# Grouping the matmuls of a half weight chunk by width in a one-layer hybrid encoder trunk

## Chip, cores and metric

The kernel runs on one core of a Trainium2 chip, as one program that is launched once. The metric is the device time of one execution in microseconds (us). The engines are named as in the profile: PE is TensorE (the matmuls), PEld its weight loads, DVE is VectorE, ACT is ScalarE, POOL is GpSimd and SP issues the DMAs.

## What is computed

One layer of an encoder trunk on 256 tokens of width 2048, all in float32:

```
h    = rmsnorm(x, norm_mix);  proj = h @ w_in            # 2048 -> 6176 columns, the mixers' inputs
y    = concat(ssd_mixer(proj), gla_mixer(proj))          # 256 x 2048
x    = x + y @ w_out                                     # output projection, 2048 -> 2048
h    = rmsnorm(x, norm_ffn)
u    = causal_dwconv3(h @ ffn_w_up)                      # 2048 -> 2 x 5632
gate, val = split(u)
x    = x + (silu(gate) * val) @ ffn_w_down               # 5632 -> 2048
pg   = sigmoid(rmsnorm(x, norm_ple) @ ple_w_gate)        # 2048 -> 2048
x    = x + pg * (p @ ple_w_proj)
out  = rmsnorm(x, norm_final)
```

The change touches the four large products with `w_out`, `ffn_w_up`, `ffn_w_down` and `ple_w_gate`, that is, everything from the output projection on.

## The kernel before

**Tiling.** Activations lie transposed in the on-chip memory: 128 channels on the partitions, the 256 tokens along the free axis. Each weight matrix is cut into blocks of 128 x 128. One product (m, k) multiplies block (m, k) by the 128 input channels k and adds into output tile m, an accumulator `pm_t` of 128 x 512 in PSUM. There are four such accumulators.

**Two parts for each number.** Weights and activations are each split into a high part and a low part (the tiles `whi` and `wlo`; an activation tile is 128 x 2 x 256, high part first, low part second), and the matmuls take these split tiles. A product is then two matmuls in `mm2`: `whi` against both activation parts side by side, 512 columns wide (line 219, or line 222 for the last k of an output tile), and `wlo` against the high part alone, 256 columns wide, added into the first half of the accumulator (line 220). For the last k the narrow one comes first and the wide one last. Each matmul loads its own weights. The input projection and one output tile of the last stage (`single`) use `mm3` instead: three matmuls of 256 columns (lines 226 to 228).

**Weight stream.** A chunk is 16 blocks, 128 x 2048, fetched by one DMA into a `raw` tile (four of them). A half chunk is 8 blocks. For each half, ACT casts `raw` into `whi` (line 185, in `prepare`) and DVE subtracts to give `wlo` (line 186). There are five `whi` and five `wlo` buffers, so a cast has to wait until PE is done with the half chunk that stood in the buffer.

**Stages.** `project` walks a list of products made by `steps`, 16 per chunk. The last four k (five in the down projection) of the first two output tiles come after both tiles' other products, so that the activations which are finished last are needed late. The stages are: the output projection (256 products), then twice the up projection (704) and down projection (352) of one half of the hidden channels, then the gate projection (256, of which the last tile's 16 use `mm3`). That makes 2624 products, 2608 of them in `mm2`.

**Order around them.** The order of PE's instructions is the order of the program text; a scheduler at build time orders the other engines. When an output tile is whole, `evac` is called: it adds to the residual (line 917) and splits the sum for the next stage (lines 260 and 261), or, in the up projection, combines the two halves of the accumulator (lines 232 and 233), does the convolution and gating (lines 957 to 969) and splits the result (lines 267 and 268). Every four products `tick()` lets one waiting task put in its next piece. Here these are a norm's small matmuls (line 288, then line 321 six ticks later, and the copy of its result, line 331) and the loads of `p @ ple_w_proj` for the gate stage.

Of the kernel before, what the change touches and what calls it, by code (L numbers as in the profile page):

```python
# [15 lines left out]
T = 256  # L16
# [28 lines left out]
TICK = 4  # L45
# [36 lines left out]


def steps(n_m, n_k, tail):
    """(m, k) in the order of the products: the last k of the first two m come after both."""
    cut = n_k - tail
    s = [(m, k) for m in (0, 1) for k in range(cut)]
    s += [(m, k) for m in (0, 1) for k in range(cut, n_k)]
    return s + [(m, k) for m in range(2, n_m) for k in range(n_k)]


SEQ16 = steps(16, KT, 4)
SEQ_UP = steps(2 * UPH, KT, 4)
SEQ_DN = steps(16, UPH, 5)


@with_exitstack
def trunk(ctx, tc, wst, wv, xin, pin, prm_d, cst_d, gku_d, out):
    nc = tc.nc
    V, S, G, PE = nc.vector, nc.scalar, nc.gpsimd, nc.tensor  # L100
# [12 lines left out]
    def slot(dtype=F32, shape=(128, 512)):  # L113
        return gpool.tile(list(shape), dtype, name="slot")
# [4 lines left out]
    def pmt():  # L119
        return pm.tile([128, 512], F32, name="pm_t")  # L120

    def pxt():
        return px.tile([128, 512], F32, name="px_t")
# [1 line left out]
    def v3(ap, n):  # L125
        return ap.rearrange("p (a b) -> p a b", a=n)

# [1 line left out]
    now = [0]  # L129
    tasks = []  # L130
    done = {}
# [1 line left out]
    def tick():  # L133
        now[0] += 1
        for t in list(tasks):
            if t[0] <= now[0]:
                d = next(t[1], None)
                if d == 0:
                    continue
                if d is None:  # L140
                    tasks.remove(t)
                else:
                    t[0] = now[0] + d
                break
# [8 lines left out]
        while any(done.get(k, 1 << 30) > now[0] for k in keys):  # L153
            yield 0

# [1 line left out]
    ready = {}  # L157

    def raw_tile():
# [37 lines left out]
    def load(c):  # L197
        if c not in ready and c < N_CHUNK:
            ci = ORDER[c]
            with tc.high_priority(offset=PRIO):  # L200
                if c not in loaded:
                    fetch_ahead(c)
                ready[c] = prepare(loaded.pop(c), ci, 1)

    def chunk(c):
        load(c)
        load(c + 1)
        return ready.pop(c)

    def lhs(wt, j):  # L210
        hi, lo = wt[j // 8]
        w = slice((j % 8) * 128, (j % 8 + 1) * 128)
        return hi[:, w], lo[:, w]

    def mm2(ps, wt, j, act, first, last):
        hi, lo = lhs(wt, j)
        both = act.rearrange("p a t -> p (a t)")
        if not last:
            PE.matmul(ps, lhsT=hi, rhs=both, start=first, stop=False)  # L219
        PE.matmul(ps[:, 0:T], lhsT=lo, rhs=act[:, 0, :], start=False, stop=False)  # L220
        if last:
            PE.matmul(ps, lhsT=hi, rhs=both, start=False, stop=True)  # L222

    def mm3(ps, wt, j, act, first, last):
        hi, lo = lhs(wt, j)
        PE.matmul(ps, lhsT=hi, rhs=act[:, 0, :], start=first, stop=False)  # L226
        PE.matmul(ps, lhsT=hi, rhs=act[:, 1, :], start=False, stop=False)  # L227
        PE.matmul(ps, lhsT=lo, rhs=act[:, 0, :], start=False, stop=last)  # L228
# [5 lines left out]
        return t  # L234

    def project(base, seq, acts, n_k, evac, single=None):
        """Products of a weight stream in the order seq; evac(m, ps) when an output tile is whole."""
        ps = {}
        wt = None
        for n, (m, k) in enumerate(seq):  # L240
            if n % 16 == 0:
                wt = chunk(base + n // 16)
            if k == 0:
                ps[m] = pmt()
            if m == single:
                mm3(ps[m][:, 0:T], wt, n % 16, acts[k], k == 0, k == n_k - 1)
            else:
                mm2(ps[m], wt, n % 16, acts[k], k == 0, k == n_k - 1)
            if k == n_k - 1:
                evac(m, ps.pop(m))  # L250
            if n % TICK == TICK - 1:
                tick()

# [1 line left out]
    def pcol(i):  # L255
        return prm[:, i:i + 1]

# [73 lines left out]
        S.copy(out=keep, in_=ps)  # L331
        then(r, keep)

# [1 line left out]
    prm = const.tile([128, NPRM], F32, name="prm")  # L335
    x = const.tile([128, KT, T], F32, name="x")
    cst = const.tile([128, NCST], F32, name="cst")
# [33 lines left out]
    for m in range(KT):  # L371
        wt = ready[m // 8]
        if m % 2 == 0:
            ps = pmt() if m % 4 == 0 else pxt()
# [19 lines left out]
    for a in proj:  # L394
        store_proj(*a)

# [1 line left out]
    usuf_r = const.tile([128, 128], F32R, name="usuf_r")  # L398
    ones_r = const.tile([128, 128], F32R, name="ones_r")
    cbh = const.tile([128, 12], F32, name="cbh")  # L400
# [38 lines left out]
        S.activation(out=t, in_=c, func=AF.Tanh)  # L439
        V.scalar_tensor_tensor(out=out, in0=t, scalar=1.0, in1=c, op0=ALU.add, op1=ALU.mult)  # L440

# [1 line left out]
    gkl = const.tile([32, T], F32, name="gkl")  # L443
    G.memset(gkl, 1.0)
    dta = const.tile([128, 32], F32, name="dta")
# [73 lines left out]
        PE.matmul(ps[:, 16:32], lhsT=tri, rhs=a_tm[:, 16:32], start=True, stop=True)  # L519
        S.activation(out=esuf, in_=ps[:, 0:32], func=AF.Exp)  # L520

# [1 line left out]
    ssd_x = [None] * 8  # L523
    bT = slot()
    cT = slot()
# [194 lines left out]
                    mix[i] = split(y)  # L720
            yield from norm_task(ssd_sq[g], 512, then, 9)

# [1 line left out]
    gq = [slot(), slot()]  # L724
    gk = [slot(), slot()]
    gla = {}
# [119 lines left out]
        V.tensor_tensor(out=o, in0=o, in1=sg, op=ALU.mult)  # L846
        mix[8 + i] = split(o)

# [1 line left out]
    def ev_in(kind, i, ps):  # L850
        if kind == "conv":
            ev_conv(i, ps)
        elif kind == "q":
            ev_qk(gq, i, ps, 128.0 ** -0.5)
        elif kind == "k":
            ev_qk(gk, i, ps, 1.0)
            mark(("k", i))
        elif kind == "z":
            ev_z(i, ps)
        else:  # L860
            ev_g(i, ps)

    vps = None
    for ci, (kind, i) in enumerate(PLAN):
        if ci == 0:
            late_loads()
        if ci > 2:
            wt = chunk(N_PROJ + ci)
        else:
            wt = ready.pop(N_PROJ + ci)  # L870
# [14 lines left out]
        if kind == "v":  # L885
# [3 lines left out]
            for kk in range(4):  # L889
                k = kc * 4 + kk  # L890
                hi, lo = wt[kk // 2]
# [11 lines left out]
        else:  # L903
            ps = pmt()
# [6 lines left out]
    while tasks:  # L911
        tick()

# [1 line left out]
    def add_res(i, ps):  # L915
        for h in range(2):
            V.tensor_tensor(out=x[:, i, :], in0=x[:, i, :], in1=ps[:, h * T:(h + 1) * T], op=ALU.add)  # L917
# [8 lines left out]
    sq_ffn = SumSq()  # L926
    xf = [None] * KT
    project(OFF_OUT, SEQ16, mix, KT, residual(sq_ffn, P_GFFN, xf))

# [1 line left out]
    state.clear()  # L931

    def delayed(f):
# [42 lines left out]
    for half in range(2):  # L976
        base = OFF_F0 if half == 0 else OFF_F1
        project(base, SEQ_UP, xf, KT, ev_up(half))
        if half == 0:
            project(base + N_UP, SEQ_DN, hid, UPH, add_res)  # L980
        else:
            sq_ple = SumSq()
            project(base + N_UP, SEQ_DN, hid, UPH, residual(sq_ple, P_GPLE, xg))

# [1 line left out]
    state.clear()  # L986
    sq_fin = SumSq()
    emb = {}
# [52 lines left out]
    start(first_emb())  # L1041
    project(OFF_GATE, SEQ16, xg, KT, delayed(ev_gate), single=KT - 1)

# [1 line left out]
    banks = {}  # L1045

    def turn(q, c):
# [19 lines left out]
    with tc.high_priority(offset=PRIO):  # L1067
        v, t = [small.tile([128, 2], F32, name=n, bufs=2) for n in ("rv", "rt")]
# [105 lines left out]
```

## Time and profile before

| | us |
|---|---|
| device time, median of 3 runs (lowest to highest) | 1256.36 (1256.25 to 1256.43) |
| span of the profiled execution | 1254.4 |
| PE busy in it | 1243.2 (99%) |
| DVE busy | 896.0 (71%) |
| ACT busy | 691.2 (55%) |
| the four large projections, from the first wide matmul to the last | 313.25 to 1235.57 |

The profiled span leaves out about 1.9 us that the device time holds around it. Matmuls are pipelined: one that is listed with 0.40 us starts 0.23 us before the next. What a matmul costs is therefore read from the distance between two starts in the timeline, not from its listed duration.

### The profile page before, as it was taken

What the parts mean: (1) busy time and instruction counts of PE and PEld (TensorE: products, weight loads), DVE (VectorE), ACT (ScalarE), POOL (GpSimd) and SP (SyncE); (2) the same over time, 40 slices, a digit from 0 to 9 for tenths busy, and PEclk for the clock granted to TensorE, in tenths of its full rate; (3) what the DMA queues carried; (4) which work ended last, traced back from release to release, by engine and by line L of the source; (5) the groups of instructions that cost most, each with busy time, mean ns of one, the idle gap of its engine ahead of it and who ended that gap; (6) DMA issues with size and microseconds to landing.
All of it is one profiled execution on the core that took longest, in us unless ns stands there. A gap on an engine that the chain in (4) does not pass through costs nothing.

```text
span 1254.4 us, 19554 instructions
## 1 busy us (share of the span) xinstructions
PE 1243.2 (99%) x7707; PEld 1110.7 (89%) x7707; DVE 896.0 (71%) x1531; ACT 691.2 (55%) x1144; POOL 2.9 (0%) x10
## 2 busy tenths in 40 slices
PE   9999999999999999999999999999999999999997
PEld 7999999999888888888888888888888888888886
DVE  7877665788777787777775555777777776666775
ACT  8685564565545565555553333555555554444664
POOL 0000000000000000000000000000000000000000
PEclk9999999999999999999999999999999999999999
DMA  9745353344555455555555555555555555556531
GB/s 332 295 156 172 124 202 135 137 167 168 198 174 199 168 202 173 196 179 191 187 183 193 178 197 174 198 173 197 183 186 191 179 196 193 199 172 223 197 131 67
DMA packets 36830, 231.01 MB, mean 184 GB/s; under 512 B 4209, under 2 KB 4593, under 8 KB 11138
## 3 DMA queue, kind: packets, MB, share of 16 engines
q1 hardware_dynamic: 36738, 229.76, 52.4%
q8 instruction: 60, 0.98, 0.3%
q14 instruction: 32, 0.26, 0.1%
HBM read 225.55 MB, written 4.19 MB: 183 GB/s over the span
## 4 chain that ended last, share of the span: by engine, by line
PE 97%; DVE 1%; ACT 1%; DMA 1%; SPq 0%; issue 0%; DVEq 0%
PE pm_t L219 46%; PE pm_t L220 25%; PE pm_t L226 6%; PE pm_t L228 6%; PE pm_t L227 6%; PE pm_t L222 3%; PE pm_t L897 1%; PE pm_t L898 1%; PE pm_t L896 1%; DMA raw<-in_wst_dram 1%; PE px_t L629 1%; DVE wlo L186 0%; PE px_t L792 0%; ACT xg L260 0%; PE px_t L288 0%; ACT whi L185 0%
## 5 line engine op out<-in xcount | busy, mean ns | idle before, releaser
L185 ACT CAST whi<-raw 128x1024 fp32r<-128x1024 f32 (+3 forms) x444 | 444.2, 1005 | 513.8 <-PE pm_t L219 244.1
L186 DVE TENSOR_TENSOR wlo<-raw,whi 128x1024 fp32r<-128x1024 f32 (+3 forms) x444 | 517.1, 1168 | 273.3 <-ACT whi L185 270.5
L219 PE MATMUL pm_t<-xg,whi 128*128 128x512 f32 x1545 | 549.8, 398 | 0.0
L220 PE MATMUL pm_t<-xg,wlo 128*128 128x256 f32 x1648 | 446.0, 281 | 0.0
L219 PEld LDWEIGHTS pm_t<-xg,whi 128*128 128x128 f32 x1545 | 290.3, 188 | 66.5
L219 PE MATMUL pm_t<-slot,whi 128*128 128x512 f32 x912 | 324.1, 398 | 0.0
L220 PEld LDWEIGHTS pm_t<-xg,wlo 128*128 128x128 f32 x1648 | 311.1, 189 | 10.1
L220 PE MATMUL pm_t<-slot,wlo 128*128 128x256 f32 x960 | 261.8, 281 | 0.0
L219 PEld LDWEIGHTS pm_t<-slot,whi 128*128 128x128 f32 x912 | 171.4, 188 | 40.2
L220 PEld LDWEIGHTS pm_t<-slot,wlo 128*128 128x128 f32 x960 | 181.3, 189 | 4.7
L226 PE MATMUL pm_t<-xg,whi 128*128 128x256 f32 x592 | 170.1, 287 | 0.0
L228 PE MATMUL pm_t<-xg,wlo 128*128 128x256 f32 x592 | 167.4, 283 | 0.0
L227 PE MATMUL pm_t<-xg,whi 128*128 128x256 f32 x592 | 167.4, 283 | 0.0
L226 PEld LDWEIGHTS pm_t<-xg,whi 128*128 128x128 f32 x592 | 113.0, 191 | 1.2 <-issue 1.0
L227 PEld LDWEIGHTS pm_t<-xg,whi 128*128 128x128 f32 x592 | 113.0, 191 | 0.5 <-issue 0.2
L228 PEld LDWEIGHTS pm_t<-xg,wlo 128*128 128x128 f32 x592 | 113.0, 191 | 0.0
L962 DVE SCALAR_TENSOR_TENSOR tmp<-tmp,prm 128x255 f32<-128x255 f32 (+1 forms) x176 | 84.5, 480 | 3.9 <-ACT tmp L959 1.0
L917 DVE TENSOR_TENSOR x<-x,pm_t 128x256 f32<-128x256 f32 x96 | 40.1, 419 | 25.7 <-PE pm_t L222 24.4
L959 ACT ACTIVATE tmp<-tmp,prm 128x256 f32<-128x256 f32 x88 | 52.4, 596 | 0.4 <-DVE tmp L957 0.4
L233 DVE TENSOR_TENSOR tmp<-pm_t,tmp 128x256 f32<-128x256 f32 x103 | 43.0, 418 | 0.7 <-ACT tmp L232 0.7
L222 PE MATMUL pm_t<-xg,whi 128*128 128x512 f32 x103 | 41.2, 400 | 0.0
L232 ACT COPY tmp<-pm_t 128x256 f32<-128x256 f32 x103 | 37.5, 364 | 1.4 <-PE pm_t L222 1.4
(210 smaller groups left out, 836.0 us busy)
## 6 DMA issues: line engine op xcount, KB each, us to landing
raw<-in_wst_dram SPq DMA_DIRECT2D x200, 1024.0 KB, 4.9
raw<-in_wv_dram SPq DMA_DIRECT2D x8, 704.0 KB, 4.1
raw<-in_wv_dram SPq DMA_DIRECT2D x8, 352.0 KB, 8.3
x<-in_xin_dram SPq DMA_DIRECT2D x4, 512.0 KB, 8.4
pp<-slot SPq DMA_DIRECT2D x8, 256.0 KB, 8.2
slot<-pp SPq DMA_DIRECT2D x8, 256.0 KB, 5.5
out_dram<-raw SPq DMA_DIRECT2D x8, 256.0 KB, 3.2
raw<-in_wst_dram SPq DMA_DIRECT2D x2, 512.0 KB, 7.4
```

The costliest lines, as they stand in the source:

```text
L185: S.copy(out=hi[:, sl], in_=raw[:, rs])
L186: V.tensor_tensor(out=lo[:, sl], in0=raw[:, rs], in1=hi[:, sl].bitcast(F32), op=ALU.subtract)
L219: PE.matmul(ps, lhsT=hi, rhs=both, start=first, stop=False)
L220: PE.matmul(ps[:, 0:T], lhsT=lo, rhs=act[:, 0, :], start=False, stop=False)
L222: PE.matmul(ps, lhsT=hi, rhs=both, start=False, stop=True)
L226: PE.matmul(ps, lhsT=hi, rhs=act[:, 0, :], start=first, stop=False)
L227: PE.matmul(ps, lhsT=hi, rhs=act[:, 1, :], start=False, stop=False)
L228: PE.matmul(ps, lhsT=lo, rhs=act[:, 0, :], start=False, stop=last)
L233: V.tensor_tensor(out=t, in0=ps[:, 0:T], in1=t, op=ALU.add)
L917: V.tensor_tensor(out=x[:, i, :], in0=x[:, i, :], in1=ps[:, h * T:(h + 1) * T], op=ALU.add)
L959: S.activation(out=c, in_=v, func=AF.Identity, scale=pcol(P_FW + 176 + ch), bias=pcol(P_FB + ch))
L962: V.scalar_tensor_tensor(out=c[:, s:], in0=v[:, :T - s], scalar=pcol(P_FW + 88 * (2 - s) + ch), in1=c[:, s:], op0=ALU.mult, op1=ALU.add)
```

## The change

`mm2` is gone. `project` first cuts its list of products into runs: neighbouring products of one output tile that lie in one half chunk, at most eight. For a run it issues all the wide matmuls (`whi`, 512 columns), then all the narrow ones (`wlo`, 256 columns), and only then the evacuation and the ticks of the run's products. Products with `mm3` keep their order. The last matmul of an output tile is now a narrow one.

```
+        runs = []
+        for n, (m, k) in enumerate(seq):
+            if runs and runs[-1][0] == m and n % 8 and len(runs[-1][1]) < 8:
+                runs[-1][1].append((n, k))
+            else:
+                runs.append((m, [(n, k)]))
...
-                mm2(ps[m], wt, n % 16, acts[k], k == 0, k == n_k - 1)
-            if k == n_k - 1:
-                evac(m, ps.pop(m))
-            if n % TICK == TICK - 1:
-                tick()
...
+                for n, k in run:
+                    PE.matmul(ps[m], lhsT=lhs(wt, n % 16)[0],
+                              rhs=acts[k].rearrange("p a t -> p (a t)"), start=k == 0, stop=False)
+                for n, k in run:
+                    PE.matmul(ps[m][:, 0:T], lhsT=lhs(wt, n % 16)[1], rhs=acts[k][:, 0, :],
+                              start=False, stop=k == n_k - 1)
+            for n, k in run:
+                if k == n_k - 1:
+                    evac(m, ps.pop(m))
+                if n % TICK == TICK - 1:
+                    tick()
```

The other lines of the diff take out comments and docstrings. The 2608 products fall into 362 runs: 292 of eight, the others of one to seven where an output tile ends inside a half chunk or where the first two tiles leave their last k for later.

PE, where one output tile of the output projection ends and the next begins, before (the wide matmuls are lines 219 and 222, the narrow ones line 220):

```order
L219 MATMUL pm_t<-slot,whi 128x512
L220 MATMUL pm_t<-slot,wlo 128x256 x2
L222 MATMUL pm_t<-slot,whi 128x512
L219 MATMUL pm_t<-slot,whi 128x512
L220 MATMUL pm_t<-slot,wlo 128x256
```

PE at the start of the output projection, after (lines 217 to 219 are the last `mm3` of the input projection; the wide matmuls are now line 247, the narrow ones line 250):

```order
L217 MATMUL pm_t<-xg,whi 128x256
L218 MATMUL pm_t<-xg,whi 128x256
L219 MATMUL pm_t<-xg,wlo 128x256
L247 MATMUL pm_t<-slot,whi 128x512 x8
L250 MATMUL pm_t<-slot,wlo 128x256 x8
L247 MATMUL pm_t<-slot,whi 128x512 x4
L250 MATMUL pm_t<-slot,wlo 128x256 x4
```

Before, wide and narrow alternate, and only where a tile ends do two of a kind meet; now they stand in rows of up to eight.

ACT at the start of the up projection, before (casts of weights, evacuation copies of line 232 and the norm's work on `diag` and `rb`):

```order
L185 CAST whi<-raw 128x1024 x3
L232 COPY tmp<-pm_t 128x256
L185 CAST whi<-raw 128x1024 x2
L313 ACTIVATE diag<-cst,rh_4940 128x128 x2
L313 ACTIVATE diag<-cst,rl_4942 128x128 x2
L185 CAST whi<-raw 128x1024
L331 COPY rb<-px_t 128x256
L185 CAST whi<-raw 128x1024
L959 ACTIVATE tmp<-tmp,prm 128x256
```

The same place after:

```order
L185 CAST whi<-raw 128x1024 x2
L223 COPY tmp<-pm_t 128x256
L185 CAST whi<-raw 128x1024 x2
L317 ACTIVATE diag<-cst,rh_4940 128x128 x2
L317 ACTIVATE diag<-cst,rl_4942 128x128 x2
L185 CAST whi<-raw 128x1024 x2
L335 COPY rb<-px_t 128x256
L963 ACTIVATE tmp<-tmp,prm 128x256
```

One cast has moved behind the first evacuation copy, and another ahead of the copy of the norm's result. Such moves by one place are found through all four projections on ACT, and on DVE where the two additions to the residual now stand on either side of a weight subtraction; the work itself is the same.

## Rows read from the trace of the kernel before

**Rows 1.** The page: engines' busy time, and the chain of work by engine.

```profile
PE 1243.2 (99%) x7707; PEld 1110.7 (89%) x7707; DVE 896.0 (71%) x1531; ACT 691.2 (55%) x1144; POOL 2.9 (0%) x10
...
PE 97%; DVE 1%; ACT 1%; DMA 1%; SPq 0%; issue 0%; DVEq 0%
```

**Rows 2.** Windows: stretch, its us, busy us by engine, clock, DMA share, GB/s.

```profile
core 0: us, PE busy (x) PEld busy (x) DVE busy (x) ACT busy (x) POOL busy (x), PEclk, DMA share, GB/s
...
313.25:1235.57 922.32, 922.32 (x5230) 800.52 (x5229) 659.12 (x1018) 482.37 (x719) 0.00 (x0) 1.00 0.53 184
1235.57:1254.40 18.83, 10.41 (x89) 10.08 (x87) 8.96 (x27) 8.54 (x20) 0.00 (x0) 0.90 0.32 111
```

**Rows 3.** The chain of work, two ends of output tiles, 16 tiles apart (start, us).

```profile
861.71 0.24 PE pm_t L220 x2
...
952.17 0.24 PE pm_t L220 x2
```

**Rows 4.** Timeline of PE in the input projection (start, us), first and last of 22.

```profile
199.76 0.28 PE L228 MATMUL pm_t<-xg,wlo 128*128 128x256 f32 x1
...
202.28 0.28 PE L228 MATMUL pm_t<-xg,wlo 128*128 128x256 f32 x1
```

**Rows 5.** Timeline of PE where an output tile ends.

```profile
861.79 0.40 PE L222 MATMUL pm_t<-xg,whi 128*128 128x512 f32 x1
862.03 0.40 PE L219 MATMUL pm_t<-xg,whi 128*128 128x512 f32 x1
862.26 0.28 PE L220 MATMUL pm_t<-xg,wlo 128*128 128x256 f32 x1
862.37 0.40 PE L219 MATMUL pm_t<-xg,whi 128*128 128x512 f32 x1
```

**Rows 6.** Timeline of PE: two wide, then ten narrow matmuls, in three places.

```profile
92.52 0.40 PE L592 MATMUL px_t<-slot,usuf_r 128*128 128x512 f32 x1
...
92.98 0.28 PE L226 MATMUL pm_t<-xg,whi 128*128 128x256 f32 x1
...
94.05 0.28 PE L226 MATMUL pm_t<-xg,whi 128*128 128x256 f32 x1
...
161.83 0.39 PE L592 MATMUL px_t<-slot,usuf_r 128*128 128x512 f32 x1
...
162.29 0.28 PE L226 MATMUL pm_t<-xg,whi 128*128 128x256 f32 x1
...
163.38 0.28 PE L226 MATMUL pm_t<-xg,whi 128*128 128x256 f32 x1
...
1235.57 0.28 PE L226 MATMUL pm_t<-xg,whi 128*128 128x256 f32 x1
...
1236.64 0.28 PE L226 MATMUL pm_t<-xg,whi 128*128 128x256 f32 x1
```

**Rows 7.** Timeline of PE: the last wide matmuls of two neighbouring output tiles.

```profile
415.18 0.40 PE L222 MATMUL pm_t<-xg,whi 128*128 128x512 f32 x1
...
420.75 0.40 PE L222 MATMUL pm_t<-xg,whi 128*128 128x512 f32 x1
```

**Rows 8.** What the weight casts of line 185 waited for, 320 to 1235 us.

```profile
  PE pm_t L219: 242.6, 188
  PE pm_t L222: 161.5, 108
```

**Rows 9.** Timeline: last activations for the gate projection, then for a down projection.

```profile
1152.79 0.48 DVE L261 SCALAR_TENSOR_TENSOR xg<-x,prm,xg 128x256 fp32r<-128x256 f32 x1
...
660.84 0.42 DVE L268 TENSOR_TENSOR slot<-tmp,slot 128x256 fp32r<-128x256 f32 x1
```

**Rows 10.** Timeline in the gate projection: evacuation copy, then the norm's matmuls and copy.

```profile
1163.25 0.37 ACT L232 COPY tmp<-pm_t 128x256 f32<-128x256 f32 x1
...
1169.03 0.40 PE L321 MATMUL px_t<-diag,ones_r 128*128 128x256 f32 x2
1169.46 0.37 ACT L331 COPY rb<-px_t 128x256 f32<-128x256 f32 x1 [0.55 <-PE px_t L321]
```

More of the change, by code (lines that the diff above doesn't have):

```diff
@@ L213, in lhs @@
         return hi[:, w], lo[:, w]
[L215 to L222, printed above, removed]
     def mm3(ps, wt, j, act, first, last):
@@ L238, in project @@
         ps = {}
+        runs = []
[4 more added lines that the diff above has]
+                runs.append((m, [(n, k)]))
         wt = None
[L240 to L243, printed above, removed]
+        for m, run in runs:
+            if run[0][0] % 16 == 0:
+                wt = chunk(base + run[0][0] // 16)
+            if run[0][1] == 0:
                 ps[m] = pmt()
             if m == single:
-                mm3(ps[m][:, 0:T], wt, n % 16, acts[k], k == 0, k == n_k - 1)
-            else:
-                mm2(ps[m], wt, n % 16, acts[k], k == 0, k == n_k - 1)
-            if k == n_k - 1:
-                evac(m, ps.pop(m))
-            if n % TICK == TICK - 1:
-                tick()
+                for n, k in run:
+                    mm3(ps[m][:, 0:T], wt, n % 16, acts[k], k == 0, k == n_k - 1)
+            else:
+                for n, k in run:
[4 more added lines that the diff above has]
+                              start=False, stop=k == n_k - 1)
+            for n, k in run:
+                if k == n_k - 1:
+                    evac(m, ps.pop(m))
+                if n % TICK == TICK - 1:
+                    tick()
     def pcol(i):
```

## The prediction

> **What bounds the kernel now.** I read the page first. TensorE is busy 99% of the span and the chain that ended last is TensorE for 97% [rows 1]. The windows then separate the part that the change touches: from 313.25 to 1235.57 us TensorE is busy for all of 922.32 us, and the granted clock is 1.00, the 2.4 GHz level [rows 2]. So no wait for weights, activations or accumulators is left in there to win; the stretch is as long as the distances between the starts of its matmuls, which the timeline shows. In 16 whole output tiles of 16 products the time is 952.17 - 861.71 = 90.46 us, or 0.3534 us for a product, that is, for one wide and one narrow matmul [rows 3]. The whole question is whether a wide one and a narrow one cost something else when they stand among their own kind. One nanosecond on each of the 2608 products is 2.6 us, 0.2% of the time.
>
> **The narrow matmuls in a row.** The input projection is a long row of 256-column matmuls, each with its own weight load: 22 of them start from 199.76 to 202.28, so 21 distances make 2.52 us, 0.1200 each [rows 4]. If a narrow matmul costs that everywhere, the wide one in alternation costs 0.3534 - 0.1200 = 0.2334. A row that has just followed a wide matmul is a little cheaper at its start. From the first narrow one to the tenth, nine distances, there are 1.07 us behind two wide ones at 92.98, 1.09 at 162.29, and 1.07 behind the wide one that ends the mixed products at 1235.57 [rows 6]; nine at 0.1200 would be 1.08. That is -10, +10 and -10 ns for a run, -3 in the mean. I take -5 ns for each of 362 runs, since two of three places have -10: **-1.8 us**, between +3.6 and -3.6.
>
> **The wide matmuls in a row.** No row of eight exists before; the nearest are pairs. Where an output tile ends, two wide ones start at 861.79 and 862.03 and the next narrow one at 862.26: 0.47 us for the two, 0.235 each [rows 5]; the 150 tile ends look like this one. In the mixer, behind narrow or 352-column matmuls, two wide ones take 92.98 - 92.52 = 0.46 and 162.29 - 161.83 = 0.46, 0.230 each [rows 6]. So the bounds are 0.230 and 0.235, with 0.2334 from the difference above between them. I take their middle, 0.2325, as the pair of the mixer follows a long narrow row, as every run will, while the pair at a tile's end has two narrow ones ahead of it. Against 0.2334 that is -0.9 ns for 2608 wide matmuls: **-2.3 us**, between -8.9 (0.230) and +4.2 (0.235).
>
> **A rule against the change.** A matmul's weights are loaded while the one before it runs. In alternation the load for a narrow matmul has a wide one to hide under; in a row of narrow ones every load has only a narrow one. The rows show 0.1200 in such a row [rows 4], and in alternation 862.37 - 862.26 = 0.11 for the narrow one behind two wide ones [rows 5]. The slower one of the rivals below is built on this mechanism.
> The Trainium skill, page "TensorE: Matmul & The Clock Gate", section "Back-to-back issue gap", says likewise that in a stream of matmuls with a load for each the spacing is set by both operations together. Its formula there for a lone matmul at the full clock, N/2.4 + 2.5 ns, would give, as an estimate, 215.8 and 109.2 ns, a pair of 0.325 us in any order and so no change; the trace has 0.3534 for the pair, so the formula's level does not hold here.
>
> **What else moves, at no cost.** The number of matmuls, weight loads, casts and DMAs stays. The two pairs at tile ends vanish into the runs; they are in the mean of [rows 3] already. A `whi` buffer is now free after the wide matmuls of its half chunk instead of at its end, a third of a half chunk earlier. The casts wait for TensorE, 242.6 and 161.5 us in all [rows 8], and TensorE never for them, so an earlier release only moves ACT's idle time; DVE's `wlo` is needed eight wide matmuls later than before. Behind a waiting cast on ACT stand the evacuations; but an accumulator is needed again only three output tiles later, 3 x 16 x 0.3534 = 17 us, and the moves by one cast of 1.05 us are small beside that. The wide matmuls ask for their activations a little earlier. The last split for the gate projection ends at 1152.79 + 0.48 = 1153.27 [rows 9]; its product is the 28th, and its wide matmul now starts 24 x 0.3534 + 3 x 0.2334 = 9.2 us behind the stage's start at 1150.32, at 1159.5: 6 us of slack. For the down projection the last split ends at 661.26 [rows 9] and is needed 34 x 0.3534 + 4 x 0.2334 = 12.9 us behind 652.88, at 665.8: 4.5 us. Ticks of a run come at its end: the norm's sum still goes in after product 28, where a run ends anyway, but its matmuls of line 321 move from behind product 52 to behind product 56, 1.4 us later. They, at 1169.03, and the copy at 1169.46 free no accumulator; the copies that do so run ahead of them, one at 1163.25 [rows 10]. On SP one load of the embedding passes one chunk fetch, with DMA engines busy for 0.53 of the time [rows 2]. Should one of these covers fail, a cast of 1.05 us comes bare, in one of the four places where a stage begins. The tail from 1235.57 on, 18.83 us [rows 2], keeps its order.
>
> **Sum.** 1254.4 - 1.8 - 2.3 = 1250.3 us of span. The median of the runs is 1256.36, 1.9 us more, which I carry over: **1252.2 us**, -0.33%. With the bounds: 1256.36 - 3.6 - 8.9 = 1243.9 to 1256.36 + 3.6 + 4.2 = 1264.2.
>
> **Rivals.**
> *Nothing happens (1256.4 us).* Wide and narrow cost 0.2334 and 0.1200 in any order, because what is lost between two matmuls depends on their widths alone. For it: inserting a pair of wide and a pair of narrow ones at a tile end leaves the mean at 0.3534, close to 0.235 + 0.1200 of [rows 4, 5]. Against it: 0.230 in the mixer, and the next rival's rows.
> *Slower: narrow runs are held by their own loads (1263.1 us).* The narrow ones take 0.1200, with no gain at the start of a run, and the wide ones keep the 0.236 that two starts in alternation can be apart (0.235 by [rows 5], where it is 0.24 and then 0.23): 0.356 against 0.3534 is 2.6 ns, times 2608 = +6.8 us. It decides from a mean of 0.3544 for a wide and a narrow one on, 1 ns above now. Against it: the pairs in the mixer.
> *Much faster: the short spacing everywhere (1239.5 us).* One output tile, behind the norm's small matmuls, has 420.75 - 415.18 = 5.57 us between its ends [rows 7] against 16 x 0.3534 = 5.65: the same products at 0.3481 or, without the tile's end, less. So the alternation itself can lose less between matmuls, and falls back at the tile's end. If runs fall into this spacing, at least 5 ns, and 6.5 if the loss of the tile's end goes too, are saved for each product: 6.5 x 2608 = 16.9 us. For it: rows of one width also keep a steady rhythm. Against it: it is rare here, a few tiles of 150.
> *The change doesn't do what it says.* It does: the order of the built program has the runs of eight; no chance is kept for this.
>
> **How the numbers follow.** My forecast, a small gain from both terms, gets 0.45; it is faster by over 0.2% (2.5 us, about what a measurement can tell from no change) in 0.36 of it, and within in 0.09. Nothing happens: 0.23. Slower: 0.18. Short spacing: 0.14. So faster 0.36 + 0.14 = 0.50, same 0.09 + 0.23 = 0.32, slower 0.18. The range reaches from the forecast's low bound, 1243.9, to 1261, which leaves out the short spacing (0.14) and the upper third of the slower case (0.06); the forecast's own range is 1243.9 to 1256.4.
>
> **What will show it.** In the timeline of the changed kernel, eight wide starts in a row: 0.230 to 0.2335 apart makes the forecast, 0.236 the slower rival, 0.227 or less the short spacing. Eight narrow starts: 0.96 us or a little less. The windows of the stretch should show TensorE busy throughout again and a length of 918 us instead of 922.3. A gap on TensorE at a stage's start, or a wait for `whi`, `wlo` or `rb` in its list of waits, would show that a cover failed. The prediction is wrong if wide matmuls among themselves lose more than pairs of them do.

## The result

| | before | after |
|---|---|---|
| device time, median us | 1256.35 | 1246.61 (1246.29 to 1247.31, 4 runs) |
| ratio after to before | | 0.9922, 95% interval 0.9908 to 0.9936 |
| span of the profiled execution | 1254.4 | 1244.6 |
| from the first wide matmul of the output projection to the end of the mixed products | 922.32 | 911.96 |
| rest up to the end | 18.83 | 19.31 |

The changed kernel is 9.7 us faster, 0.78%. The page of the changed kernel, first engines and then the chain of work (compare [rows 1]):

```profile
PE 1233.3 (99%) x7707; PEld 1113.4 (89%) x7707; DVE 894.4 (72%) x1531; ACT 691.3 (56%) x1144; POOL 3.0 (0%) x10
...
PE 95%; ACT 2%; DVE 1%; DMA 1%; issue 0%; SPq 0%; DVEq 0%; ACTq 0%
```

The windows of the changed kernel (stretch, its us, busy us of each engine, clock, DMA share, GB/s; compare [rows 2]):

```profile
313.33:1225.29 911.96, 911.96 (x5230) 802.41 (x5229) 656.39 (x1016) 482.28 (x719) 0.00 (x0) 1.00 0.53 186
1225.29:1244.60 19.31, 10.43 (x90) 10.10 (x88) 10.03 (x29) 8.67 (x21) 0.00 (x0) 0.86 0.31 109
```

The gain lies in the four projections alone: 922.32 - 911.96 = 10.4 us with TensorE busy throughout in both kernels, at the same granted clock. Nothing that waited has gone; the same matmuls start closer to each other. By kind, the mean distances from one start to the next in this stretch, worked out from the trace's start times, went from 236.1 to 230.3 ns behind a wide matmul and from 117.1 to 118.9 ns behind a narrow one: -15.1 and +4.8 us. The tail gives 0.5 us back. Two runs of eight, from the timeline of TensorE in the first up projection (start, length, x count; a row begins at the first matmul of its run):

```profile
501.18 2.00 PE L247 MATMUL pm_t<-xg,whi 128*128 128x512 f32 x8
503.02 1.11 PE L250 MATMUL pm_t<-xg,wlo 128*128 128x256 f32 x8
503.98 2.00 PE L247 MATMUL pm_t<-xg,whi 128*128 128x512 f32 x8
```

Eight wide ones take 503.02 - 501.18 = 1.84 us, 0.230 each; eight narrow ones 0.96, 0.120 each. Together 2.80 us for eight products, 0.350 against 0.3534 in [rows 3]. The same timeline, opened a little later so that a row begins inside the run:

```profile
502.57 0.62 PE L247 MATMUL pm_t<-xg,whi 128*128 128x512 f32 x2
503.02 0.52 PE L250 MATMUL pm_t<-xg,wlo 128*128 128x256 f32 x3
```

The last two of the eight take 503.02 - 502.57 = 0.45, 0.225 to 0.23 each. Over all 292 whole runs the mean distances by place are, in ns, worked out from the trace's start times: wide 233.3, 235.6, 228.4, 232.4, 230.7 and then three times 226.7; narrow 113.3, 119.2 and then six times 120.0. A run of wide ones starts near the spacing of alternation and settles at a lower one from its sixth on.

### The profile page after: what moved, and what is told of

Same layout as the page of the kernel before. It is cut to its first block, busy times and chain, and to the rows that moved or that the text cites. A ratio compares the mean times of both kernels' runs of the same rounds, so it can differ in the third digit from the quotient of the medians.

```text
span 1244.6 us, 19477 instructions
## 1 busy us (share of the span) xinstructions
PE 1233.3 (99%) x7707; PEld 1113.4 (89%) x7707; DVE 894.4 (72%) x1531; ACT 691.3 (56%) x1144; POOL 3.0 (0%) x10
## 4 chain that ended last, share of the span: by engine, by line
PE 95%; ACT 2%; DVE 1%; DMA 1%; issue 0%; SPq 0%; DVEq 0%; ACTq 0%
PE pm_t L247 48%; PE pm_t L250 25%; PE pm_t L217 6%; PE pm_t L218 6%; PE pm_t L219 6%; PE pm_t L901 1%; PE pm_t L902 1%; PE pm_t L900 1%; DMA raw<-in_wst_dram 1%; PE px_t L633 1%; ACT whi L185 0%; ACT tmp L285 0%; ACT xg L264 0%; PE px_t L796 0%; DVE wlo L186 0%
## 5 line engine op out<-in xcount | busy, mean ns | idle before, releaser
L185 ACT CAST whi<-raw 128x1024 fp32r<-128x1024 f32 (+3 forms) x444 | 443.8, 1004 | 500.7 <-PE pm_t L247 383.4
L247 PE MATMUL pm_t<-xg,whi 128*128 128x512 f32 x1648 | 413.9, 392 | 0.0
L247 PEld LDWEIGHTS pm_t<-xg,whi 128*128 128x128 f32 x1648 | 296.0, 189 | 52.5
L247 PE MATMUL pm_t<-slot,whi 128*128 128x512 f32 x960 | 245.3, 392 | 0.0
L250 PEld LDWEIGHTS pm_t<-xg,wlo 128*128 128x128 f32 x1648 | 225.6, 190 | 16.6
L250 PE MATMUL pm_t<-xg,wlo 128*128 128x256 f32 x1648 | 230.7, 282 | 0.0
L219 PE MATMUL pm_t<-xg,wlo 128*128 128x256 f32 x592 | 167.4, 283 | 0.0
L250 PEld LDWEIGHTS pm_t<-slot,wlo 128*128 128x128 f32 x960 | 134.7, 190 | 11.7
L250 PE MATMUL pm_t<-slot,wlo 128*128 128x256 f32 x960 | 138.4, 282 | 0.0
L217 PEld LDWEIGHTS pm_t<-xg,whi 128*128 128x128 f32 x592 | 113.0, 191 | 1.2 <-issue 1.0
L218 PEld LDWEIGHTS pm_t<-xg,whi 128*128 128x128 f32 x592 | 113.0, 191 | 0.4 <-issue 0.2
L219 PEld LDWEIGHTS pm_t<-xg,wlo 128*128 128x128 f32 x592 | 113.0, 191 | 0.0
L961 DVE TENSOR_TENSOR tmp<-tmp,rb 128x256 f32<-128x256 f32 x88 | 37.1, 421 | 1.4
```

The source lines that it names most:

```text
L185: S.copy(out=hi[:, sl], in_=raw[:, rs])
L247: PE.matmul(ps[m], lhsT=lhs(wt, n % 16)[0], rhs=acts[k].rearrange("p a t -> p (a t)"), start=k == 0, stop=False)
L250: PE.matmul(ps[m][:, 0:T], lhsT=lhs(wt, n % 16)[1], rhs=acts[k][:, 0, :], start=False, stop=k == n_k - 1)
```

## The experiments

At this point there were two theories. Mine: the distance between two starts depends on what stands in a row, each place of a run having its price. The rival: something else in the change makes the gain, since it also moves evacuation and ticks to the end of a run, frees `whi` earlier and makes the last matmul of an output tile a narrow one. The first four kernels separate these.

**Everything but the grouping.** The narrow matmul moves up into the loop of the wide one, so that the two alternate; the run, its evacuation and its ticks stay as in the changed kernel.

```
                 for n, k in run:
                     PE.matmul(ps[m], lhsT=lhs(wt, n % 16)[0],
                               rhs=acts[k].rearrange("p a t -> p (a t)"), start=k == 0, stop=False)
-                for n, k in run:
                     PE.matmul(ps[m][:, 0:T], lhsT=lhs(wt, n % 16)[1], rhs=acts[k][:, 0, :],
                               start=False, stop=k == n_k - 1)
```

> The changed kernel, but inside a run wide and narrow alternate as before; evacuation, ticks and the narrow last matmul stay as in the changed kernel. Theory (distance between starts depends on what stands in a row): the pair is back at 0.3534 us, time 1256.4 us, within 0.2% of the kernel before. Rival (the gain comes from the moved evacuation and ticks, the earlier whi buffers, or the last matmul of a tile being narrow): time as the changed kernel, 1246.6 us.

Measured: 1243.21 us, 0.9894 (0.9880 to 0.9909) of the kernel before, and 3.4 us faster than the changed kernel. My theory failed here: without any grouping the gain is larger. Windows of this kernel:

```profile
313.83:1221.19 907.36, 907.36 (x5231) 792.96 (x5230) 657.74 (x1015) 481.98 (x716) 0.00 (x0) 1.00 0.54 187
```

The starts in its trace are as far apart as before, 236.6 ns behind a wide and 116.7 behind a narrow matmul in the mean, up to 413 us, and then 231.7 and 115.0 for the whole rest. So alternation has two spacings, 353.3 and 346.7 ns a product. The short output tile of [rows 7], one of four in the kernel before, had the second of them.

The change is thereby split in two. Without the grouping the stretch falls from 922.32 to 907.36 us; the grouping on top of that, in the changed kernel, lengthens it again by 4.6 us to 911.96. Only in the first 100 us, where this kernel still has 353.3 ns a product, are the runs of eight the faster ones, with 349.3.

**The length of the runs.** The limit of eight becomes 2, 4 or 16 in both places of the line; for 2:

```
-            if runs and runs[-1][0] == m and n % 8 and len(runs[-1][1]) < 8:
+            if runs and runs[-1][0] == m and n % 2 and len(runs[-1][1]) < 2:
```

> The changed kernel with runs of at most two products. Theory (the first wide matmuls behind narrow ones cost 0.233 to 0.236, only from the sixth on 0.2267; the first two narrow ones 0.1133 and 0.1192): 0.7014 us for two products, 0.3507 each, 2.6 ns below before, time 1249.5 us; with the changed kernel's own 16 runs of two (0.4692 + 0.2282 us) 1244.3 us. Rival (each width has one price among its own kind, 0.2300 and 0.1191, at any length): 1245.4 us.

Measured: 1244.40 us, 0.9903 (0.9887 to 0.9920).

> The changed kernel with runs of at most four products. Theory (price by place in the run): 0.2333+0.2356+0.2284+0.2324 + 0.1133+0.1192+0.1200+0.1200 = 1.4022 us, 0.3506 a product, time 1249.1 us; by the changed kernel's own runs of four (0.9342 + 0.4732 us) 1252.5 us. Rival (one price for each width): 1245.4 us.

Measured: 1251.00 us, 0.9957 (0.9943 to 0.9972).

> The changed kernel with runs of up to 16 products, a whole chunk. Theory (price by place): eight more wide matmuls at 0.2267 and eight more narrow ones at 0.1200 behind the first eight: 1.8404+1.8134+0.9525+0.9600 = 5.5663 us for 16, 0.3479 a product against 0.3491 in runs of eight, time 1243.5 us where all runs were whole. Rival (one price for each width): 1246.6 us as with runs of eight; a third: the narrow parts or buffers held longer make TensorE wait, over 1247 us, with gaps on TensorE in the windows.

Measured: 1246.31 us, 0.9919 (0.9904 to 0.9934). Runs of 2 beat runs of 4, so the rival with one price for each width, 1245.4 for both, is out. The prices by place, taken from runs of eight, gave 1249.1 for runs of 4, 2 us too little, and 1249.5 for runs of 2, 5 us too much. The second forecast, from the few short runs of the changed kernel itself, gave 1252.5 for runs of 4, 1.5 us too much, and 1244.3 for runs of 2, as measured. So what a matmul costs depends on more than its place in the run: in runs of 2 the two wide distances are 233.1 and 233.3 ns and the narrow ones 114.6 and 115.8, in runs of eight the first two of each are 233.3 and 235.6, 113.3 and 119.2. Runs of 2, from the timeline of TensorE:

```profile
500.35 0.63 PE L247 MATMUL pm_t<-xg,whi 128*128 128x512 f32 x2
500.82 0.39 PE L250 MATMUL pm_t<-xg,wlo 128*128 128x256 f32 x2
501.05 0.62 PE L247 MATMUL pm_t<-xg,whi 128*128 128x512 f32 x2
501.51 0.40 PE L250 MATMUL pm_t<-xg,wlo 128*128 128x256 f32 x2
501.74 0.63 PE L247 MATMUL pm_t<-xg,whi 128*128 128x512 f32 x2
```

Four products in 501.74 - 500.35 = 1.39 us, 0.3475 each by two digits and 0.3484 in the mean of all. In runs of 4 the rows are:

```profile
500.22 1.09 PE L247 MATMUL pm_t<-xg,whi 128*128 128x512 f32 x4
501.15 0.63 PE L250 MATMUL pm_t<-xg,wlo 128*128 128x256 f32 x4
501.62 1.09 PE L247 MATMUL pm_t<-xg,whi 128*128 128x512 f32 x4
```

That is 1.40 us for four, 0.350 each by two digits and 0.3509 in the mean of all; the whole stretch took 916.07 us against 909.82 in runs of 2.

With runs of 16 the price by place held: 16 wide ones take 507.68 - 504.03 = 3.65 us and 16 narrow ones 1.92, from the timeline of TensorE.

```profile
504.03 3.82 PE L247 MATMUL pm_t<-xg,whi 128*128 128x512 f32 x16
507.68 2.08 PE L250 MATMUL pm_t<-xg,wlo 128*128 128x256 f32 x16
509.60 2.68 PE L247 MATMUL pm_t<-xg,whi 128*128 128x512 f32 x11
```

From the sixth wide one on they are 226.7 ns apart in the mean. The stretch is 2.6 us shorter than with runs of eight, but the time is not. Windows and TensorE's list of waits (who waited, for whom, us in all, times, longest) for this kernel behind the mixed products:

```profile
314.01:1223.34 909.33, 909.33 (x5230) 802.87 (x5229) 649.88 (x1014) 493.26 (x716) 0.00 (x0) 1.00 0.54 187
1223.34:1244.80 21.46, 12.34 (x90) 11.78 (x88) 11.09 (x31) 9.51 (x23) 0.00 (x0) 0.82 0.28 98
```

```profile
PE px_t L1062 <- DVE acc L286: 1.0, 1, 1.0
PE px_t L1063 <- DVE tmp L1035: 0.9, 1, 0.9
```

The tail of 21.46 us against 19.31 with runs of eight gives most of the gain back: the last norm waits for the sums of squares on DVE, which is still busy with the tiles before the last one. In this execution the stretch also begins 0.7 us later. In the changed kernel the same list has one row, in the kernel before none:

```profile
PE px_t L1063 <- DVE tmp L1035: 0.5, 1, 0.5
```

**A new theory.** Alternation has a long and a short rhythm, and which one it runs in is a state: it stays until something breaks the row of matmuls. The norm's small matmuls bring the short one, and the turned pairs at the ends of output tiles, narrow narrow wide wide, bring the long one back. Three kernels test it on the kernel before, with its evacuation and ticks in place.

*No turned pairs.* The last k goes wide first, as every other one does:

```
-        if not last:
-            PE.matmul(ps, lhsT=hi, rhs=both, start=first, stop=False)
-        PE.matmul(ps[:, 0:T], lhsT=lo, rhs=act[:, 0, :], start=False, stop=False)
-        if last:
-            PE.matmul(ps, lhsT=hi, rhs=both, start=False, stop=True)
+        PE.matmul(ps, lhsT=hi, rhs=both, start=first, stop=False)
+        PE.matmul(ps[:, 0:T], lhsT=lo, rhs=act[:, 0, :], start=False, stop=last)
```

> The kernel before with one edit: the last k of an output tile also goes wide first, narrow last, so wide and narrow alternate without a break; evacuation and ticks stay where they were. Theory (alternation has two rhythms, 0.3533 and 0.3467 us a product; the norm's small matmuls at 413 us bring the short one, and a turned pair at a tile's end brings the long one back): long up to 413 us, short for the 2324 products behind it, 15.5 us less, 1241 to 1243 us as with the alternating kernel with moved ticks. Rival (the moved evacuation and ticks made that kernel fast): 1256.4 us.

Measured: 1241.54 us, 0.9881 (0.9866 to 0.9896). This alone is faster than the changed kernel, whose interval, 0.9908 to 0.9936, does not reach it. The timeline of TensorE around the norm's small matmuls (line 285 here; wide is line 218, narrow line 219):

```profile
412.27 0.40 PE L218 MATMUL pm_t<-xg,whi 128*128 128x512 f32 x1
412.51 0.28 PE L219 MATMUL pm_t<-xg,wlo 128*128 128x256 f32 x1
412.63 0.40 PE L218 MATMUL pm_t<-xg,whi 128*128 128x512 f32 x1
...
412.99 0.50 PE L285 MATMUL px_t<-cst,acc 128*128 128x1 f32 x4
...
413.78 0.40 PE L218 MATMUL pm_t<-xg,whi 128*128 128x512 f32 x1
414.01 0.28 PE L219 MATMUL pm_t<-xg,wlo 128*128 128x256 f32 x1
414.13 0.39 PE L218 MATMUL pm_t<-xg,whi 128*128 128x512 f32 x1
```

Ahead of them two wide starts are 0.36 apart, behind them 0.35. Two wide starts with 100 products between them settle it: first this kernel, later in the up projection, 634.84 - 600.17 = 34.67 us, 0.3467 each.

```profile
600.17 0.40 PE L218 MATMUL pm_t<-xg,whi 128*128 128x512 f32 x1
...
634.84 0.40 PE L218 MATMUL pm_t<-xg,whi 128*128 128x512 f32 x1
```

The stretch takes 907.35 us, that of the kernel that alternates with moved evacuation and ticks 907.36. The tail is back at 18.80 us, near the 18.83 of the kernel before, while that other kernel has 20.11, with two waits for DVE of 0.9 and 0.2 us. The windows of this kernel:

```profile
312.65:1220.00 907.35, 907.35 (x5231) 792.89 (x5229) 658.88 (x1018) 483.11 (x719) 0.00 (x0) 1.00 0.54 187
1220.00:1238.80 18.80, 10.41 (x90) 10.08 (x88) 9.12 (x27) 8.55 (x20) 0.00 (x0) 0.84 0.32 112
```

The tail of the other one:

```profile
1221.19:1241.30 20.11, 10.66 (x90) 10.10 (x88) 10.34 (x30) 9.50 (x23) 0.00 (x0) 0.87 0.30 104
```

*One turned pair in the whole kernel*, at tile 10 of the first up projection; the next kernel has two, with `m in (10, 11)` in the same line. `mm2`, not shown, puts the narrow matmul first only for the last k of a tile for which `turn_tile` is set:

```
+                turn_tile[0] = base == OFF_F0 and n_k == KT and m == 10
```

> The kernel without turned pairs, but with one turned pair at the end of the 11th output tile of the first up projection, about 470 us. Theory (the rhythm is a state that stays until something breaks the alternation): short from 414 us to that tile, 148 products, then long again up to the norm's small matmuls of the gate stage, then short for 212: 360 x 6.67 ns = 2.4 us less than before, 1254.0 us. Rival (a turned pair costs only at its own place): as without any, 1241 to 1243 us.

Measured: 1243.03 us, 0.9891 (0.9875 to 0.9908). The expectation of 1254.0 was wrong. One turned pair does not end the short rhythm; behind it the distances are 230.0 and 116.7 ns, another form with the same sum. The norm's matmuls at 1147 us then brought the *long* one, 236.0 and 117.3 ns up to the end, so they do not always bring the short one either. Wide starts with 100 products between them, behind the turned pair and behind that norm, are 634.74 - 600.08 = 34.66 and 1200.43 - 1165.11 = 35.32 us apart:

```profile
600.08 0.39 PE L222 MATMUL pm_t<-xg,whi 128*128 128x512 f32 x1
...
634.74 0.39 PE L222 MATMUL pm_t<-xg,whi 128*128 128x512 f32 x1
...
1165.11 0.40 PE L222 MATMUL pm_t<-xg,whi 128*128 128x512 f32 x1
...
1200.43 0.40 PE L222 MATMUL pm_t<-xg,whi 128*128 128x512 f32 x1
```

> As the kernel with one turned pair, but the 12th output tile of the first up projection ends with a turned pair too. In the kernel before, the first turned pair behind the norm's small matmuls left the short rhythm in place for a tile (415.18 to 420.75 us) and the second ended it. Theory (the rhythm is a state, and the second turned pair 16 products behind the first brings the long one, which then stays without further turned pairs): 0.3533 us a product from about 472 us up to the gate stage's norm, some 1960 products, 13 us more than with one or none, 1254 to 1255 us, or 1255 to 1256 if the norm does not bring the short one back. Rival (long spacing needs turned pairs all along): 1241 to 1244 us.

Measured: 1254.78 us, 0.9985 (0.9975 to 0.9994). Two turned pairs, four matmuls in another order among 5216, cost 13.2 us against none. Its timeline over 100 products from the same time on as above (wide is line 222): 635.45 - 600.11 = 35.34 us, 0.3534 each, 130 us behind the second pair and with no further one.

```profile
600.11 0.40 PE L222 MATMUL pm_t<-xg,whi 128*128 128x512 f32 x1
...
635.45 0.40 PE L222 MATMUL pm_t<-xg,whi 128*128 128x512 f32 x1
```

The long rhythm, too, stays by itself. In the kernel before, a turned pair brought it back soon behind each of the two norms.

The start times hold more than the theory did: the short rhythm has two forms, which explains the wrong expectation of 1254.0. The first has 231.7 and 115.0 ns in the mean, the second a steady 230.0 and 116.7. In both kernels the first turned pair leads from the first form to the second, and in the kernel with two the second pair leads from there to the long rhythm. The kernel before takes the same two steps behind the norm at 413 us; the tile of [rows 7] is the second form. The norm's four one-column matmuls led from the long rhythm to the first form wherever they met it, left the first form in place (at 1146 us without turned pairs), and led from the second form to the long rhythm (with one turned pair). A turned pair that meets the long rhythm mostly leaves it; two of the kernel before, at 432.26 and 1178.90 us, began a short tile, which the next pair ended.

*Setting the rhythm on purpose.* Without turned pairs, the output projection still runs in the long rhythm up to the first norm. Four small matmuls go in behind its 28th product:

```
+            if base == OFF_OUT and n == 27:
+                nudge = pxt()
+                for c in (0, 1, 0, 1):
+                    PE.matmul(nudge[:, c:c + 1], lhsT=ident, rhs=ones[:, 0:1], start=True,
+                              stop=True)
```

> The kernel without turned pairs, with four extra one-column matmuls into an accumulator that nobody reads, behind the 28th product of the output projection, the place in the stage where the norms have theirs. Theory (they set the rhythm as the norm's do): 0.3467 us a product from about 324 us on, another 228 x 6.67 ns = 1.5 us less than without them, less some 0.4 us for themselves. If they leave the long rhythm, the time is that without them plus 0.4 us; the timeline tells it.

Measured: 1241.50 us, 0.9882 (0.9868 to 0.9897), the same as without them. The timeline shows that they did what was expected of the rhythm; the four are eight matmuls on TensorE and cost 325.21 - 324.40 = 0.81 us, twice what was expected:

```profile
323.34 0.40 PE L218 MATMUL pm_t<-slot,whi 128*128 128x512 f32 x1
323.58 0.28 PE L219 MATMUL pm_t<-slot,wlo 128*128 128x256 f32 x1
323.69 0.40 PE L218 MATMUL pm_t<-slot,whi 128*128 128x512 f32 x1
...
324.40 0.95 PE L251 MATMUL px_t<-cst 128*128 128x1 f32 x8
325.21 0.48 PE L218 MATMUL pm_t<-slot,whi 128*128 128x512 f32 x1
```

From 325 us on the wide starts are 346.7 ns apart in the mean. The stretch came to 906.56 us against 907.35, and a tail of 19.53 against 18.80 took that back.

## Why the prediction was right, and where not

**The side and the range.** Faster by over 0.2% was the likeliest case, and 1246.6 lies in the range. Half of the reason held: TensorE was full before and after, and wide matmuls among themselves start closer together than they did. The forecast took 4.1 us off the stretch, to 918, and the trace shows 10.4. That the mean of a run is the 0.230 which the prediction read from the mixer's pairs [rows 6] is luck. By the unrounded start times those pairs take 0.467 and 0.462 us; a run starts with 0.469 for two, and only its later places bring the mean down to 0.230.

**The wide term was too small.** It was to be 0.2325 a matmul, -2.3 us. Measured are 0.2300 in whole runs, 3.4 ns below 0.2334; that would be -8.9 us for 2608. But 0.2334 was no measured distance. It is what is left of 0.3534 if a narrow matmul takes 0.1200 in alternation too; there it takes 0.1171 and the wide one 0.2361. So the wide ones gained 5.8 ns and the narrow ones lost 1.8. The other step that failed is the bound: I took pairs as the nearest rows and a middle between two kinds of pairs, as if the second wide matmul of a run stood for the eighth. A run settles only from its sixth, at 0.2267, below both bounds. [Rows 7] held the sum to which a run settles: inside that tile a product takes 0.3467, though as 0.2300 and 0.1167. I kept it for a rival with 0.14.

**The narrow term.** -5 ns for a run was taken, -7.5 measured in whole runs against eight at 0.1200 (0.9525 against 0.9600 us); against the 0.1171 of alternation it is a loss. The expected mechanism is there: the first narrow one behind a wide one has 113.3 ns. The slower rival was half right: narrow matmuls do cost more in a row, the 0.1200 that [rows 4] already had, but the wide ones did not keep the 0.236 of alternation; they are at 0.2300. Whether the narrow ones' own loads set the 0.1200 was not tried. A wide and a narrow one at the end of their runs, 226.7 + 120.0, make 346.7 ns, exactly the short rhythm of alternation. Nothing in the runs lies below that sum for long.

**What else moves.** No wait for weights, activations or accumulators appeared: the list of TensorE's waits for the stretch is empty in the changed kernel as it was before. ACT's casts still wait for TensorE, with 383.4 us for line 247 against 404.1 before [rows 8], as expected. One cover failed, the tail: "18.83 us, keeps its order" is true for TensorE, but it is 0.5 us longer through the wait for DVE shown above. The runs of 16, with 1.0 and 0.9 us, show that wait growing. The two kernels that alternate without turned pairs tell where it comes from: with evacuation and ticks at the end of a run the tail is 20.11 us, with both in their old place 18.80. So it does not take the grouping of the matmuls; which of the moved pieces delays the last evacuations was not tried by itself.

**A right answer with half the reason.** "Nothing happens" argued that a loss depends on widths alone; the prediction argued that it depends on neighbours. The experiments show a third thing: it depends on a rhythm that outlasts its cause by hundreds of microseconds. The kernel before stood in the long rhythm nearly throughout, and the runs with none, one and two turned pairs tie that to those pairs. The changed kernel has next to no alternation that could fall into it, four runs of one product. It is not the best cure: alternation without turned pairs reaches 346.7 ns, runs of eight 349.1. The prediction put the turned pairs that "vanish into the runs" at nothing, and this step failed: taking them out alone is worth 15.0 us of the stretch, 922.32 to 907.35. The grouping, from which the whole gain was to come, costs 4.6 us against alternation without them. Against the long rhythm it does gain, as the first 100 us show, 349.3 against 353.3 ns. So the side was right for a reason that the prediction had only in part. Grouped matmuls with a turned pair left at each tile's end were not run.

**Open.** What in TensorE holds the rhythm, and why a break leads from one form to just that other one, is not settled. In these runs the order of the matmuls decided it. Nothing in the traces ties it to the other engines: the 0.3467 and 0.3534 stay steady over hundreds of products beside changing work on ACT and DVE.

## What to carry to other kernels

When TensorE is busy throughout, compare the distances between starts in several places of the trace before an order is costed, and take a place with a shorter distance for the same instructions as a target, however rare it is. A stream of one fixed pattern should be kept free of small breaks, such as a last step in another order; here, taking the turned pair out, the smallest edit of all, gave 1.2%, more than the regrouping with 0.8%. After a gain of a few us, look at the tail too, since the next engine may be late there.

## What the runs showed of the hardware

- Alternating 512- and 256-column matmuls, each with its own weight load, run at 353.3 or 346.7 ns a pair at the full granted clock; both persist, and two pairs in another order switched the short one to the long one at a price of 13.2 us in this kernel.
- In rows of one width, 256-column matmuls settle at 120.0 ns and 512-column ones at 226.7 ns. The difference of 106.7 ns for 256 columns is 0.417 ns a column, one period of the clock at its 2.4 GHz level; by this estimate 13.3 ns of either distance do not depend on the width.
- A row of wide ones behind narrow ones needs five matmuls to settle; a row of narrow ones begins with a shorter distance than it settles at.
